# A gated-linear-attention block on one core: weight parts of w_in kept in DRAM after the first block of tokens, and w_o's scaled rows prepared in the last block

## The chip, the cores and the metric

One core of one Trainium2 chip runs the whole program. The metric is the device time of one execution in microseconds; the time of a kernel is the median of its runs. The core's engines are TensorE (PE, with its weight loads as PEld), VectorE (DVE), ScalarE (ACT), GpSimd (POOL) and SyncE (SP), which here issues nearly all transfers, and 16 DMA engines behind the queues.

## The reference, cut to what matters

One layer over 2048 latent tokens of width 1024, with 256 context tokens before them. Attention is gated linear attention in both directions, 4 heads with keys of 128 and values of 256, in chunks of 64 tokens; a two-layer MLP of width 4096 with a squared ReLU follows.

```python
def gla_mixer(a_ctx, a_lat, w_in, w_a1, w_a2, b_a, g_head, w_o, need_ctx):
    def project(a):
        q, k, v, r = jnp.split(a @ w_in, [GLA_DK, 2 * GLA_DK, 2 * GLA_DK + GLA_DV], axis=-1)
...
    def finish(o, r):
        B, T = o.shape[:2]
        o = head_rmsnorm(o, g_head).reshape(B, T, GLA_DV).astype(r.dtype)
        return (o * jax.nn.silu(r)) @ w_o
...
    h_lat = h_lat + mod_l[2] * o_lat
    h_lat = h_lat + mod_l[5] * sqrelu_mlp(modulate(rmsnorm(h_lat, norm2_g[i]), mod_l[3], mod_l[4]), mlp_w1[i], mlp_w2[i])
```

`w_in` is 1024 x 3072, `w_o` 1024 x 1024. `g_head` scales the rows of `w_o`, and the residual factor `mod_l[2]` its columns. The vectors `mod_l` come from a product with `ada_w` (1024 x 6144).

## The kernel before

Every product of two float32 matrices is made of three products of halves (`mm3`, L83 to L86): each operand X is split into a high part, X rounded to the matmul's float32 form by an ACT cast, and a low part, X minus its high part. L84 multiplies high by high, L85 and L86 high by low and low by high. A weight that goes into a product therefore needs two operations after its load: the cast and the subtraction.

The program has a start (modulation vectors, first tokens), attention's first stage, its second stage, and the MLP. The first stage (the loop over `seq`, L443) goes backwards over four blocks of tokens; block 0 holds the context and two halves of 256 latent tokens, blocks 1 to 3 two halves each. In each block it goes over the 4 heads. A head takes three pieces of `w_in`, each 1024 x 256, through `load_piece`: "qk" (L451), "v" (L464) and "r" (L550). On PE a head runs as follows: keys and queries of both halves (`kqps`), a transpose of the decayed keys (`ptk`, L502) that waits for DVE's `kr` (L497), the values of the first half (`vps`), the transpose for the second half, its values, and then for each 128 tokens the state update `pu_`, the gate product `rps` and the output `pov`. `pov` waits for DVE's `st` (L579).

`load_piece` is called 48 times, so each of the 12 pieces of `w_in` is loaded and split four times, once for each block. A call loads two halves of 512 KB (`wraw`), casts each on ACT (L343, `wh`) and subtracts on POOL (L345, `wl`); only the very first half is subtracted on DVE. The tiles `wh` and `wl` have two buffers each, `wraw` has four.

Beside the heads, DVE adds up products of `ada_w` for the modulation vectors (`awp` into `acc`, L627 to L631, six rows of 128 x 512 for each head, from the second head on to the twelfth).

At the start of the second stage (L668 to L680) `w_o` is loaded in eight tiles of 128 x 1024 (`wor`), multiplied on DVE by the rows' head factor `gh` and the columns' residual factor `g1t` (L676), cast on ACT (L677) and subtracted (L678) on DVE and POOL in turn. In the same stretch the output of chunk 0, the last one of the backward pass, is finished (`finish0`, L433; `turn0` with its transposes `pt`, L104), and PE multiplies it by `w_o` (`yp`). Then the second stage goes over the chunks: `front` makes a chunk's attention output (`st` L702, `pov`), and the projection by `w_o` and what prepares the MLP follow.

A list scheduler puts each engine's instructions in order when the program is built; pools with a fixed number of buffers set when a load may be issued. All loads here go through SP's queue, in SP's order.

Of the kernel before, what the change touches and what calls it, by code (L numbers as in the profile page):

```python
# [8 lines left out]
F32 = mybir.dt.float32  # L9
# [4 lines left out]
ALU = mybir.AluOpType  # L14
# [3 lines left out]
P = 128  # L18
D = 1024
ND = D // P  # L20
# [3 lines left out]
NH = 4  # L24
HK = 128
HV = 256
# [11 lines left out]
def kernel(  # L38
# [21 lines left out]
    nc = tc.nc  # L60
# [3 lines left out]
    w_in, w_a1, w_a2, b_a, w_o = w_in[0], w_a1[0], w_a2[0], b_a[0], w_o[0]  # L64

    cmn = ctx.enter_context(tc.tile_pool(name="cmn", bufs=1))
    dram = ctx.enter_context(tc.tile_pool(name="dram", bufs=1, space=DRAM))
# [10 lines left out]
    hs_d = dram.tile([NB, 7, 2, P, NFP, 256], F32, name="hs_d")  # L78
    wt_d = dram.tile([4, NFP, P, 512], F32, name="wt_d")
    g_d = dram.tile([2, P, D], F32, name="g_d")  # L80


    def mm3(ps, sh, sl, mh, ml, start, stop, skip=False):  # L83
# [58 lines left out]
    ab_sh1, ab_sc1, n1g, n2g, gh, ab_sh2, ab_sc2 = (vec[:, 2 + i] for i in range(NV - 2))  # L142
# [6 lines left out]
    def held(shape, dtype, name, n):  # L149
        return [hold.tile([P] + shape, dtype, tag="hb", name=name) for _ in range(n)]  # L150
# [10 lines left out]
    with ExitStack() as sa:  # L161
# [7 lines left out]
        one = sa.enter_context(tc.tile_pool(name="a_one", bufs=1))  # L169
# [45 lines left out]
        for half in range(2):  # L215
            pada = pm.tile([P, 2, hk_, 4], F32, tag="m", name="pada")
            for part in range(2):
# [4 lines left out]
                for q_ in range(2):  # L222
                    c0 = part * D + half * 512 + q_ * 256
# [18 lines left out]
                for j in range(hk_):  # L242
# [9 lines left out]
                                           op0=ALU.add, op1=ALU.mult)  # L252
# [75 lines left out]

        n_piece = [0]

        def load_piece(cols):
            n_piece[0] += 1
            wh = wp.tile([P, ND, 256], F32R, tag="wh", name="wh")
            wl = wp.tile([P, ND, 256], F32R, tag="wl", name="wl")
            for half in range(2):
                raw = ld.tile([P, ND // 2, 256], F32, tag="ld", name="wraw")
                n = 256 // len(cols)
                for i, c0 in enumerate(cols):
                    nc.sync.dma_start(
                        raw[:, :, i * n:(i + 1) * n],  # L340
                        w_in[half * 512:(half + 1) * 512, c0:c0 + n].rearrange("(k p) e -> p k e", p=P))
                hs = wh[:, half * 4:half * 4 + 4, :]
                nc.scalar.copy(hs, raw)  # L343
                eng = nc.vector if (n_piece[0], half) in ((1, 0),) else nc.gpsimd
                eng.tensor_sub(wl[:, half * 4:half * 4 + 4, :], raw, hs.bitcast(F32))  # L345
            return wh, wl


# [25 lines left out]
        blocks = [[("ctx", cx, 0, 0, 1), ("lat", x, 1792, 14, 0), ("lat", x, 1536, 12, 0)]]  # L374
# [13 lines left out]
        def prep(b, hi, xs=None, ready=False):  # L388
            if b < len(blocks):
                _, src, t0, _, mi = blocks[b][hi]  # L390
                prepped[b, hi] = prep_half(src, t0, mi, xs, ready)
# [7 lines left out]
        def ada_finish(part, n, acc):  # L399
            if part in (2, 5):  # L400
                ab = one.tile([1, 512], F32, tag="adl", name="ab", bufs=3)
                e0 = part * D + n * 512
                nc.sync.dma_start(ab, ada_b[e0:e0 + 512].unsqueeze(0))
                nc.vector.tensor_add(acc[0:1], acc[0:1], ab)
                gt_ = one.tile([P, 512], F32, tag="adl", name="gt_", bufs=3)
                pg = pm.tile([P, 512], F32, tag="m", name="pg")
                nc.tensor.matmul(pg, ones, acc, start=True, stop=True)
                nc.scalar.copy(gt_, pg)
                nc.sync.dma_start(g_d[0 if part == 2 else 1, :, n * 512:(n + 1) * 512], gt_)
            else:  # L410
                ks = slice(4 * n, 4 * n + 4)
                pg = pm.tile([P, 4], F32, tag="m", name="pgc")
                for k in range(4):
                    nc.tensor.matmul(pg[:, k:k + 1], acc[:, k * P:(k + 1) * P], ones[:, 0:1], start=True, stop=True)
                if part == 3:
                    nc.vector.tensor_add(b2[:, ks], pg, ab_sh2[:, ks])
                else:
                    nc.vector.tensor_add(s2[:, ks], pg, ab_sc2[:, ks])
                    nc.vector.scalar_tensor_tensor(s2[:, ks], s2[:, ks], 1.0, n2g[:, ks], op0=ALU.add, op1=ALU.mult)
# [21 lines left out]
        acc = None  # L441
        pend = None
        for si, (b, h) in enumerate(seq):  # L443
# [4 lines left out]
                pend = [zchain(prepped[b_, hi][2][0:98], h_) for (b_, hi, h_) in zargs(b, h)]  # L448
            Es = pend
            pend = []  # L450
            wqh, wql = load_piece([h * HK, NH * HK + h * HK])  # L451

            pkq = []
            for hi, (kind, _, _, _, _) in enumerate(blk):
                ah, al, _ = pr[hi]
                ps = pj.tile([P, 2, 2, P], F32, tag="pj", name="kqps")
                for i in range(2 if kind == "lat" else 1):
                    o_ = ps[:, i].rearrange("p c j -> p (c j)")
                    c0 = HK * (1 - i)
                    for k in range(ND):  # L460
                        mm3(o_, wqh[:, k, c0:c0 + HK], wql[:, k, c0:c0 + HK], row(ah, k), row(al, k),
                            k == 0, k == ND - 1)
                pkq.append(ps)
            wvh, wvl = load_piece([2 * NH * HK + h * HV])  # L464
            vt = []

            def project_v(hi):
# [79 lines left out]
            nxt = zargs(*seq[si + 1]) if si + 1 < len(seq) else []  # L547
            if h == NH - 1 and b == 0:
                prep(b + 1, 0)
            wrh, wrl = load_piece([2 * NH * HK + NH * HV + h * HV])  # L550
            nz = 0
            for ci, (hi, kind, j, ch) in enumerate(chs):
                fb, kt, qh, at = ent[hi, j]
# [17 lines left out]
                else:  # L571
                    ah, al, _ = pr[hi]
                    rps = pj.tile([P, HV], F32, tag="pj", name="rps")
                    for k in range(ND):
# [5 lines left out]
                                                   op0=ALU.mult, op1=ALU.subtract)  # L580
# [10 lines left out]
                    else:  # L591
# [6 lines left out]
                                                       op0=ALU.mult, op1=ALU.subtract)  # L598
# [11 lines left out]
                if nz < len(nxt) and ci % 2 == 1 and (h < NH - 1 or ci >= len(chs) - 3):  # L610
                    b_, hi_, h_ = nxt[nz]
                    pend.append(zchain(prepped[b_, hi_][2][0:98], h_))
                    nz += 1
            while nz < len(nxt):
                b_, hi_, h_ = nxt[nz]
# [6 lines left out]
            for part, n, k in ada_q[6 * (si - 1):6 * si] if si else ():  # L622
                if k == 0:
                    acc = one.tile([P, 512], F32, tag="acc", name="acc")
# [7 lines left out]
                if k == ND - 1:  # L632
                    ada_finish(part, n, acc)


    nc.vector.tensor_tensor(ff[:, :, 1:], fl[:, :, :NCC + NCH - 1], fm[:, :, 1:], op=ALU.mult)

# [20 lines left out]
    with ExitStack() as sb:  # L658
# [7 lines left out]
        po = sb.enter_context(tc.tile_pool(name="b_po", bufs=2, space=PSUM, reuse_waits="tile"))  # L666

        wot = [[wo.tile([P, D], F32R, name=f"wo{i}{k}") for i in range(2)] for k in range(ND)]  # L668
        g1t, = held([D], F32, "g1t", 1)
        nc.sync.dma_start(g1t, g_d[0])  # L670
        woh, wol = [], []
        for k in range(ND):
            a_, b_ = wot[k]
            raw, = held([D], F32, "wor", 1)
            nc.sync.dma_start(raw, w_o[k * P:(k + 1) * P, :])
            nc.vector.scalar_tensor_tensor(raw, raw, gh[:, k:k + 1], g1t, op0=ALU.mult, op1=ALU.mult)  # L676
            nc.scalar.copy(a_, raw)  # L677
            (nc.gpsimd if k % 2 else nc.vector).tensor_sub(b_, raw, a_.bitcast(F32))  # L678
            woh.append(a_)
            wol.append(b_)  # L680

# [328 lines left out]
    with ExitStack() as sm:  # L1010
# [54 lines left out]
        for b in range(NB):  # L1065

            acc = [[None] * 4 for _ in range(2)]
            ssqs = [None] * 4
            for i in (1, 2, 6, 5, 3, 7, 4):
                w2 = []  # L1070
                for q in range(2):
                    yps = [py.tile([P, 512], F32, tag="y", name="yp") for _ in range(2)]
                    for fq in range(NFP // FQ):
# [4 lines left out]
                        for f in range(FQ):  # L1078
                            wh, wl = w2[fq * FQ + f]
# [73 lines left out]
```

## Time and profile before

| | |
|---|---|
| median of 3 runs | 2373.53 us (2372.31 to 2375.57) |
| profiled execution | 2376.45 us, span of the trace 2374.7 us |
| mean granted TensorE clock | 0.987 |
| busy share of the span: PE, DVE, ACT, POOL | 96%, 68%, 52%, 22% |
| POOL's subtractions L345 | 236.3 us |
| start / block 0 / blocks 1 to 3 of the first stage | 0 to 62 / 62 to 250 / 250 to 866 us |
| boundary of the stages / second stage / MLP | 866 to 902 / 902 to 1120 / 1120 to 2374.7 us |

A span counts from the first instruction to the last; the execution's own time is 1.75 us more. PE is busy nearly all the time, so the table says only that what can be won lies in PE's idle stretches and in stretches in which it runs at a lower clock; where these are has to be read stage by stage.

### The profile page before, as it was taken

How to read it: one execution, taken by the hardware profiler on the slowest of the kernel's cores; microseconds unless marked ns; L12 is line 12 of the kernel's file. 1: busy time of each engine (PE TensorE's matmuls, PEld its weight loads, DVE VectorE, ACT ScalarE, POOL GpSimd, SP SyncE). 2: the span in 40 equal slices, each digit the busy share in tenths (PEclk: the TensorE clock that was granted, in tenths of full speed). 3: DMA queues.
4: the chain of work that ended last, by engine and by line, in shares of the span. 5: the costliest groups of instructions: out<-in, count | busy, mean ns of one | idle time of the engine just before them, and what ended most of it. 6: DMA issues, size and time to landing. Idle time of an engine off the chain costs nothing.

```text
span 2374.7 us, 36202 instructions
## 1 busy us (share of the span) xinstructions
PE 2286.9 (96%) x13250; PEld 2007.2 (85%) x13250; DVE 1612.1 (68%) x2410; ACT 1232.6 (52%) x2223; POOL 532.4 (22%) x658
## 2 busy tenths in 40 slices
PE   6999999999999989999899999999999999999998
PEld 4899999999999977887688887888878888888886
DVE  7855777777676577877866668766655458745484
ACT  6544454555555556654655556555554345444351
POOL 3333335343443433421000000000002113211131
PEclk9999999999999999999999999999999999999999
DMA  9222454454443256785966668765676557756472
GB/s 280 86 90 89 147 174 147 160 157 141 150 148 109 96 187 222 248 270 196 293 204 211 212 211 271 223 217 187 214 273 245 193 170 269 279 183 221 173 263 83
DMA packets 364635, 456.82 MB, mean 192 GB/s; under 512 B 23164, under 2 KB 268996, under 8 KB 364456
## 3 DMA queue, kind: packets, MB, share of 16 engines
q1 hardware_dynamic: 361784, 446.14, 56.9%
q0 software_dynamic: 2416, 8.07, 1.1%
q8 instruction: 104, 1.70, 0.3%
q14 instruction: 75, 0.61, 0.1%
q10 hardware_dynamic: 256, 0.29, 0.0%
HBM read 318.10 MB, written 136.31 MB: 191 GB/s over the span
## 4 chain that ended last, share of the span: by engine, by line
PE 47%; DMA 2%; DVE 1%; ACT 1%; SPq 0%; issue 0%; POOL 0%; DVEq 0%; POOLq 0%; ACTq 0%
PE yp L86 9%; PE yp L84 9%; PE yp L85 9%; PE pa L84 4%; PE pa L86 4%; PE pa L85 4%; PE pb L84 2%; PE pb L86 2%; PE pb L85 2%; DMA traw<-t_d 1%; PE pc L86 1%; PE pc L84 1%; PE pc L85 1%; DMA w2r<-in_mlp_w_dram 1%; DVE ht L858 0%
## 5 line engine op out<-in xcount | busy, mean ns | idle before, releaser
L84 PE MATMUL yp<-w,hs 128*128 128x512 f32 x896 | 349.2, 390 | 3.5 <-ACT hs L1040 3.5
L86 PE MATMUL yp<-w,hs 128*128 128x512 f32 x896 | 349.4, 390 | 1.1 <-DVE hs L1041 1.1
L85 PE MATMUL yp<-w,hs 128*128 128x512 f32 x896 | 349.0, 390 | 0.0
L1032 POOL TENSOR_TENSOR w<-w2r,w 128x512 fp32r<-128x512 f32 x56 | 99.5, 1776 | 1034.8 <-ACT w L1031 1034.5
L345 POOL TENSOR_TENSOR wl<-wraw,wh 128x1024 fp32r<-128x1024 f32 x95 | 236.3, 2509 | 211.3 <-ACT wh L343 211.3
L1041 DVE TENSOR_TENSOR hs<-hsr,hs 128x1024 fp32r<-128x1024 f32 x112 | 140.2, 1255 | 136.5 <-ACT hs L1040 136.2
L1040 ACT CAST hs<-hsr 128x1024 fp32r<-128x1024 f32 x112 | 117.3, 1049 | 180.3 <-PE yp L86 154.8
L84 PEld LDWEIGHTS yp<-w,hs 128*128 128x128 f32 x896 | 168.7, 188 | 38.9 <-ACT hs L1040 3.9
L86 PEld LDWEIGHTS yp<-w,hs 128*128 128x128 f32 x896 | 168.6, 188 | 36.4 <-DVE hs L1041 1.5
L85 PEld LDWEIGHTS yp<-w,hs 128*128 128x128 f32 x896 | 168.6, 188 | 35.0
L1031 ACT CAST w<-w2r 128x512 fp32r<-128x512 f32 x224 | 137.2, 620 | 106.5 <-PE yp L86 76.8
L1032 DVE TENSOR_TENSOR w<-w2r,w 128x512 fp32r<-128x512 f32 x168 | 134.3, 814 | 59.4 <-ACT w L1031 56.3
L84 PE MATMUL vps<-wh,ah 128*128 128x256 f32 x576 | 165.7, 288 | 0.4 <-DVE qr L509 0.4
L85 PE MATMUL vps<-wl,ah 128*128 128x256 f32 x576 | 165.4, 287 | 0.0
L86 PE MATMUL vps<-wh,al 128*128 128x256 f32 x576 | 164.2, 285 | 0.0
L84 PE MATMUL kqps<-ah,wh 128*128 128x256 f32 x544 | 155.8, 286 | 0.0
L85 PE MATMUL kqps<-al,wh 128*128 128x256 f32 x544 | 154.8, 285 | 0.0
L86 PE MATMUL kqps<-ah,wl 128*128 128x256 f32 x544 | 154.1, 283 | 0.5 <-DVE wl L345 0.5
L84 PE MATMUL pa<-ht,w 128*128 128x512 f32 x384 | 150.4, 392 | 3.7 <-DVE z L981 2.0
L85 PE MATMUL pa<-ht,w 128*128 128x512 f32 x384 | 150.0, 391 | 0.0
L86 PE MATMUL pa<-ht,w 128*128 128x512 f32 x384 | 150.0, 391 | 0.0
L84 PE MATMUL rps<-wh,ah 128*128 128x256 f32 x512 | 146.1, 285 | 0.0
(1278 smaller groups left out, 6385.8 us busy)
## 6 DMA issues: line engine op xcount, KB each, us to landing
hsr<-hs_d SPq DMA_DIRECT2D x112, 512.0 KB, 4.3
w2r<-in_mlp_w_dram SPq DMA_DIRECT2D x160, 256.0 KB, 4.9
wraw<-in_gla_w_in_dram SPq DMA_DIRECT2D x64, 512.0 KB, 3.8
w1r<-in_mlp_w_dram SPq DMA_DIRECT2D x64, 512.0 KB, 4.6
hs_d<-z SPq DMA_DIRECT2D x128, 256.0 KB, 3.9
w2r<-wt_d SPq DMA_DIRECT2D x128, 256.0 KB, 4.0
hs_d<-hs SPq DMA_DIRECT2D x96, 256.0 KB, 3.2
sp_d<-sp SPq DMA_DIRECT2D x60, 384.0 KB, 2.3
```

The source lines that it names most:

```text
L84: nc.tensor.matmul(ps, sh, mh, start=start, stop=False, skip_group_check=skip)
L85: nc.tensor.matmul(ps, sh, ml, start=False, stop=False, skip_group_check=skip)
L86: nc.tensor.matmul(ps, sl, mh, start=False, stop=stop, skip_group_check=skip)
L345: eng.tensor_sub(wl[:, half * 4:half * 4 + 4, :], raw, hs.bitcast(F32))
L1031: nc.scalar.copy(w_[:, 0], raw)
L1032: (nc.vector if f % 4 else nc.gpsimd).tensor_sub(w_[:, 1], raw, w_[:, 0].bitcast(F32))
L1040: nc.scalar.copy(h_[:, 0], raw)
L1041: nc.vector.tensor_sub(h_[:, 1], raw, h_[:, 0].bitcast(F32))
```

## The change

In block 0 a piece is loaded and split as before, and its two parts are stored in DRAM (`wp_d`, 1 MB each). In blocks 1 to 3 the parts are loaded from there, in two transfers of 1 MB, straight into `wh` and `wl`, with no cast and no subtraction. In block 3, tiles of `w_o` (128 x 512, 16 of them) are loaded, multiplied on DVE by head and residual factor and stored in `wo_d`; the second stage loads these and only casts and subtracts them, all subtractions on DVE.

```diff
+    wo_d = dram.tile([ND, P, D], F32, name="wo_d")
+
+    wp_d = dram.tile([NH, 3, 2, P, ND, 256], F32, name="wp_d")
...
-        def load_piece(cols):
+        def load_piece(b, h, i):
             n_piece[0] += 1
             wh = wp.tile([P, ND, 256], F32R, tag="wh", name="wh")
             wl = wp.tile([P, ND, 256], F32R, tag="wl", name="wl")
+            if b > 0:
+                for j, w_ in enumerate((wh, wl)):
+                    nc.sync.dma_start(w_.bitcast(F32), wp_d[h, i, j])
+                return wh, wl
...
                 hs = wh[:, half * 4:half * 4 + 4, :]
                 nc.scalar.copy(hs, raw)
                 eng = nc.vector if (n_piece[0], half) in ((1, 0),) else nc.gpsimd
                 eng.tensor_sub(wl[:, half * 4:half * 4 + 4, :], raw, hs.bitcast(F32))
+            for j, w_ in enumerate((wh, wl)):
+                nc.sync.dma_start(wp_d[h, i, j], w_.bitcast(F32))
             return wh, wl
...
+            if b == len(blocks) - 1:
+                ns = slice(h // 2 * 512, (h // 2 + 1) * 512)
+                if h % 2 == 0:
+                    g1h = one.tile([P, 512], F32, tag="acc", name="g1h")
+                    nc.sync.dma_start(g1h, g_d[0, :, ns])
+                for k in range(4 * (h % 2), 4 * (h % 2) + 4):
+                    fold = one.tile([P, 512], F32, tag="adl", name="fold", bufs=3)
+                    nc.sync.dma_start(fold, w_o[k * P:(k + 1) * P, ns])
+                    nc.vector.scalar_tensor_tensor(fold, fold, gh[:, k:k + 1], g1h, op0=ALU.mult, op1=ALU.mult)
+                    nc.sync.dma_start(wo_d[k, :, ns], fold)
...
-        g1t, = held([D], F32, "g1t", 1)
-        nc.sync.dma_start(g1t, g_d[0])
         woh, wol = [], []
         for k in range(ND):
             a_, b_ = wot[k]
             raw, = held([D], F32, "wor", 1)
-            nc.sync.dma_start(raw, w_o[k * P:(k + 1) * P, :])
-            nc.vector.scalar_tensor_tensor(raw, raw, gh[:, k:k + 1], g1t, op0=ALU.mult, op1=ALU.mult)
+            nc.sync.dma_start(raw, wo_d[k])
             nc.scalar.copy(a_, raw)
-            (nc.gpsimd if k % 2 else nc.vector).tensor_sub(b_, raw, a_.bitcast(F32))
+            nc.vector.tensor_sub(b_, raw, a_.bitcast(F32))
```

On SP, in block 3 of the first stage, the order of one head's transfers before; `wraw` are halves of pieces (a qk half comes as two transfers 128x4x128), `q_d` and `sp_d` are stores of queries and of chunk results:

```order
L519 DMA q_d<-qh 128x2x128 x2
L339 DMA wraw<-in_gla_w_in_dram 128x4x256 x2
L519 DMA q_d<-qh 128x2x128
L339 DMA wraw<-in_gla_w_in_dram 128x4x256 x2
L590 DMA sp_d<-sp 128x768 x3
L339 DMA wraw<-in_gla_w_in_dram 128x4x128 x4
```

And after the change, for a head of block 2 that has no `awp` rows either (the first two `wh`, `wl` are the r piece of this head, the next two the next head's qk, the last two the next head's v):

```order
L530 DMA q_d<-qh 128x2x128 x2
L341 DMA wh<-wp_d 128x2048
L341 DMA wl<-wp_d 128x2048
L530 DMA q_d<-qh 128x2x128 x2
L341 DMA wl<-wp_d 128x2048
L341 DMA wh<-wp_d 128x2048
L601 DMA sp_d<-sp 128x768 x3
L341 DMA wl<-wp_d 128x2048
L601 DMA sp_d<-sp 128x768
L341 DMA wh<-wp_d 128x2048
```

Each head still has three pieces, in six transfers of 1 MB. A part goes straight into a buffer that PE reads, so its transfer waits for PE's last use of the piece two before it; a `wraw` transfer waited for ACT and POOL to be done with the half that was two pieces before.

On DVE, at the boundary between the two stages, before:

```order
L604 COPY o_9075<-pov 128x256
L678 TENSOR_TENSOR wo_11049<-wor,wo_11048 128x1024
L676 SCALAR_TENSOR_TENSOR wor<-wor,vec,g1t 128x1024
L433 SCALAR_TENSOR_TENSOR o_9075<-o_9075,rsr,o_9076 128x256
L676 SCALAR_TENSOR_TENSOR wor<-wor,vec,g1t 128x1024
L678 TENSOR_TENSOR wo_11053<-wor,wo_11052 128x1024
L676 SCALAR_TENSOR_TENSOR wor<-wor,vec,g1t 128x1024
L678 TENSOR_TENSOR wo_11057<-wor,wo_11056 128x1024
L676 SCALAR_TENSOR_TENSOR wor<-wor,vec,g1t 128x1024
L678 TENSOR_TENSOR wo_11061<-wor,wo_11060 128x1024
L702 SCALAR_TENSOR_TENSOR st<-xf_102,ff,st 128x256
```

The same place on DVE after the change (L615, L697, L444 and L721 are the old L604, L678, L433 and L702):

```order
L615 COPY o_8927<-pov 128x256
L697 TENSOR_TENSOR wo_10903<-wor,wo_10902 128x1024
L444 SCALAR_TENSOR_TENSOR o_8927<-o_8927,rsr,o_8928 128x256
L697 TENSOR_TENSOR wo_10905<-wor,wo_10904 128x1024
L697 TENSOR_TENSOR wo_10907<-wor,wo_10906 128x1024
L697 TENSOR_TENSOR wo_10909<-wor,wo_10908 128x1024
L697 TENSOR_TENSOR wo_10911<-wor,wo_10910 128x1024
L697 TENSOR_TENSOR wo_10913<-wor,wo_10912 128x1024
L697 TENSOR_TENSOR wo_10915<-wor,wo_10914 128x1024
L697 TENSOR_TENSOR wo_10917<-wor,wo_10916 128x1024
L721 SCALAR_TENSOR_TENSOR st<-xf_104,ff,st 128x256
```

The multiplications are gone from here (they stand, as 16 smaller ones, in the first two heads of block 3), and the four subtractions that POOL made have come to DVE. PE's order differs in few places, none of them past the boundary.

## Rows read from the trace of the kernel before

**Rows 1.** Three stretches: length, busy PE PEld DVE ACT POOL, clock, DMA share, GB/s.
```profile
62.00:250.00 188.00, 178.96 (x1439) 176.24 (x1438) 117.07 (x199) 94.21 (x177) 68.86 (x120) 0.97 0.29 94
250.00:866.00 616.00, 602.45 (x4976) 597.52 (x4975) 437.45 (x692) 326.29 (x624) 238.56 (x293) 0.99 0.43 140
866.00:902.00 36.00, 27.47 (x110) 20.47 (x109) 32.18 (x37) 19.85 (x36) 15.76 (x13) 0.81 0.76 265
```
**Rows 2.** PE's waits in blocks 1 to 3: us in total, times, longest.
```profile
PE ptk L502 <- DVE kr L497: 7.9, 5, 2.0
PE pov L85 <- DVE st L579: 2.5, 1, 2.5
PE pu L284 <- DVE al L279: 2.2, 4, 0.8
```
**Rows 3.** Timeline of all engines before one wait: start, duration, instruction.
```profile
461.58 5.62 POOL L345 TENSOR_TENSOR wl<-wraw,wh 128x1024 fp32r<-128x1024 f32 x2 [4.12 <-ACT wh L343]
...
462.05 2.90 DVE L631 SCALAR_TENSOR_TENSOR acc<-awp,sil,acc 128x512 f32<-128x512 f32 x1
...
465.58 3.75 DVE L631 SCALAR_TENSOR_TENSOR acc<-awp,sil,acc 128x512 f32<-128x512 f32 x3
...
469.25 0.68 DVE L497 TENSOR_TENSOR kr<-kqps,ge 128x512 f32<-128x512 f32 x1
...
470.07 0.63 PE L502 MATMUL ptk<-ident,kr 128*128 128x128 f32 x4 [1.93 <-DVE kr L497]
```
**Rows 4.** Instructions on `awp`, 40 to 110 us: ns min/median/max.
```profile
L631 DVE SCALAR_TENSOR_TENSOR acc<-awp,sil,acc x7: 739/742/761, 57.9 to 76.6; 128x512 f32<-128x512 f32 x7
```
**Rows 5.** Busy time by stretch, around two waits of PE.
```profile
292.00:300.00 8.00, 6.83 (x45) 6.83 (x46) 6.94 (x13) 4.33 (x9) 0.84 (x1) 0.79 0.61 194
...
470.00:476.00 6.00, 5.92 (x38) 5.96 (x39) 4.71 (x10) 2.13 (x4) 0.00 (x0) 0.72 0.78 234
```
**Rows 6.** Groups by line in blocks 1 to 3: busy us, mean ns.
```profile
L345 POOL TENSOR_TENSOR wl<-wraw,wh 128x1024 fp32r<-128x1024 f32 x74 | 184.7, 2519 | 149.5 <-ACT wh L343 149.5
...
L343 ACT CAST wh<-wraw 128x1024 fp32r<-128x1024 f32 x74 | 77.7, 1054 | 17.9 <-PE kqps L85 16.3 <-POOL flb L493 1.6
```
**Rows 7.** PE's timeline at one head's turns, in block 3.
```profile
734.88 0.28 PE L86 MATMUL rps<-wh,al 128*128 128x256 f32 x1
...
748.17 0.36 PE L84 MATMUL vps<-wh,ah 128*128 128x256 f32 x1
...
762.78 0.28 PE L84 MATMUL rps<-wh,ah 128*128 128x256 f32 x1
```
**Rows 8.** DMA issues of the page: KB each, median us to landing.
```profile
wraw<-in_gla_w_in_dram SPq DMA_DIRECT2D x64, 512.0 KB, 3.8
```
**Rows 9.** Busy time in four us of the boundary.
```profile
872.00:876.00 4.00, 1.56 (x5) 1.26 (x6) 4.00 (x2) 2.29 (x3) 4.00 (x2) 0.68 1.08 409
```
**Rows 10.** PE's waits at the boundary, 866 to 902 us.
```profile
PE pt L104 <- DVE o L433: 3.3, 1, 3.3
PE yp L85 <- DVE wo L678: 2.4, 3, 1.3
PE pov L85 <- DVE st L702: 2.0, 2, 1.7
```
**Rows 11.** Timeline of the boundary: start, duration, instruction.
```profile
871.75 4.86 POOL L678 TENSOR_TENSOR wo<-wor,wo 128x1024 fp32r<-128x1024 f32 x2
871.81 2.58 DVE L433 SCALAR_TENSOR_TENSOR o<-o,rsr,o 128x256 f32<-128x256 f32 x1 [0.72 <-POOL rsr L95]
874.31 3.39 DVE L676 SCALAR_TENSOR_TENSOR wor<-wor,vec,g1t 128x1024 f32<-128x1024 f32 x1
...
877.62 1.21 DVE L678 TENSOR_TENSOR wo<-wor,wo 128x1024 fp32r<-128x1024 f32 x1
878.75 1.27 DVE L676 SCALAR_TENSOR_TENSOR wor<-wor,vec,g1t 128x1024 f32<-128x1024 f32 x1
...
885.62 2.98 DVE L702 SCALAR_TENSOR_TENSOR st<-xf,ff,st 128x256 fp32r<-128x256 f32 x2
```

More of the change, by code (lines that the diff above doesn't have):

```diff
@@ L334, in load_piece @@
             wl = wp.tile([P, ND, 256], F32R, tag="wl", name="wl")
+            if b > 0:
+                for j, w_ in enumerate((wh, wl)):
+                    nc.sync.dma_start(w_.bitcast(F32), wp_d[h, i, j])
+                return wh, wl
+            cols = ((h * HK, NH * HK + h * HK), (2 * NH * HK + h * HV,), (2 * NH * HK + NH * HV + h * HV,))[i]
             for half in range(2):
@@ L337, in load_piece @@
                 n = 256 // len(cols)
-                for i, c0 in enumerate(cols):
+                for m, c0 in enumerate(cols):
                     nc.sync.dma_start(
-                        raw[:, :, i * n:(i + 1) * n],
+                        raw[:, :, m * n:(m + 1) * n],
                         w_in[half * 512:(half + 1) * 512, c0:c0 + n].rearrange("(k p) e -> p k e", p=P))
@@ L450 @@
             pend = []
-            wqh, wql = load_piece([h * HK, NH * HK + h * HK])
+            wqh, wql = load_piece(b, h, 0)
             pkq = []
@@ L463 @@
                 pkq.append(ps)
-            wvh, wvl = load_piece([2 * NH * HK + h * HV])
+            wvh, wvl = load_piece(b, h, 1)
             vt = []
@@ L549 @@
                 prep(b + 1, 0)
-            wrh, wrl = load_piece([2 * NH * HK + NH * HV + h * HV])
+            wrh, wrl = load_piece(b, h, 2)
             nz = 0
```

## Prediction

> **What bounds the kernel now.** The windows by stage come first. TensorE is busy nearly everywhere, so time can come only from where it is idle or runs at a lower clock. In blocks 1 to 3 PE is busy 602.45 of 616 us [rows 1]: 13.55 us idle, and a granted clock of 0.99 whose second decimal hides some 5 us more (below). At the boundary PE is busy 27.47 of 36 us at a clock of 0.81: 8.5 us idle and 0.19 x 36 = 6.8 us lost to the clock, 15.4 together [rows 1]. The DMA engines are at 0.43 in blocks 1 to 3 [rows 1], so there is room for more bytes there.
>
> The second view is the list of PE's waits in blocks 1 to 3. Nearly all of the idle time is behind DVE: 7.9 us in five waits for `kr`, 2.5 us in one for `st`, 2.2 us in four for `al` [rows 2]. DVE is busy only 437 of 616 us [rows 1], so its load does not explain that; what is late is late for a moment.
>
> The third view, the timeline before one of these waits, shows the moment [rows 3]. POOL makes two subtractions L345 between 461.58 and 467.20. In that time one accumulation on DVE takes 2.90 us, and the next three take 3.75 together. Elsewhere the same instruction takes 742 ns [rows 4]. So four accumulations that need 3.0 us took 6.65; `kr`, behind them on DVE, starts at 469.25 instead of some 3.7 us earlier, and PE, which waited 1.93 us, would not have waited at all. The other `kr` waits and the one for `st` look the same: a POOL subtraction of 4.7 to 5.6 us lies over the DVE instructions just before. So instructions on different engines, none of which waits for a result of the other, take longer while they run together. The Trainium skill, "SBUF — State Buffer" (section "SBUF: two separate sides"), states that VectorE and GpSimd share one pair of ports as an exclusive lock, held for a whole instruction, when VectorE has two SBUF inputs and GpSimd reads SBUF. The trace agrees: 2.90 us is about one L345 (2.52 us mean [rows 6]) plus a part of the normal 0.74.
>
> The stalls cost twice. After two of them the granted clock falls: 0.72 over 470 to 476 us, 0.79 over 292 to 300 us [rows 5], that is 0.28 x 6 and 0.21 x 8, 1.7 us lost after each. A third place, at 564 to 572 us, is alike. Three times 1.7 is 5.1 us.
>
> **The change part by part.**
> *Blocks 1 to 3, what goes.* Of 74 POOL subtractions there (184.7 us) and 74 casts on ACT (77.7 us) [rows 6], 72 of each go: POOL loses about 180 us and ACT 76. Neither is time of PE. What it brings is that nothing long is left on POOL: 7.9 for `kr`, 2.5 for `st` and 0.8 of the 2.2 for `al` (the one of the four that lies under a POOL subtraction) are 11.2 us of waits [rows 2], and with them the 5.1 us of low clock. Upper bound 16.3 us. For the lower bound I leave half of the `kr` waits and one low-clock stretch standing (4 + 1.7), which gives 10.6. I take 15, since the row shows a margin of 1.8 us (3.7 against 1.93) for the wait that I worked out.
>
> *Blocks 1 to 3, what is added.* Six transfers of 1 MB for each head in place of raw halves: 36 MB become 72 MB. 140 GB/s over 616 us becomes about 200 [rows 1], far from the 409 that the boundary reaches [rows 9]. The point is when they may start: a part goes straight into a buffer that PE still reads. In one head [rows 7] the r piece can start when `kqps` is done (748) and is needed at 762.78: 14.8 us. The next v piece starts when `rps` is done (735) and is needed at 748.17: 13 us, and its second transfer stands behind a store of the last chunk, an estimated 2 us later (the nine products of the last `pov` and its copy), so 11 us are left. The next qk piece has more than the r piece. No row has a 1 MB transfer. From below: 512 KB land in 3.8 us [rows 8], and 0.52 MB more at 409 GB/s [rows 9] take 1.3, so 5.1 us for the first and 7.7 for two in a row. From above: 3.8 us for 512 KB [rows 8] four times one after the other, 15.2 us, if nothing overlaps. At the boundary's 409 GB/s transfers do overlap (512 KB in 3.8 us alone are 138 GB/s), so I take 7.7; against 11 it is hidden, with 3 us to spare, and so costs nothing. If that cover goes, each head loses what is missing and a low-clock stretch on top. By the fit of the Trainium skill, "DMA: Bandwidth & Descriptors" (section "Anatomy of one DMA"), 2.0 us plus bytes over 436 GB/s, one after the other, two 1 MB transfers take 8.8 us; the sum would be the same, with 2 us to spare in place of 3.
>
> *Block 0.* 24 MB of stores come onto SP's queue. The store of `wl` waits for POOL's subtraction, and behind it stand the raw loads of the piece after next, which wait for the same subtraction anyway. 94 GB/s [rows 1] plus 24 MB in 188 us make about 220. POOL's subtractions stay, and with them the 9 us idle [rows 1]. Cost 0, bounds 3 either way.
>
> *The products of w_o in block 3.* 16 accumulations' worth of DVE, 0.74 us each by the nearest row [rows 4], are 12 us beside a DVE that has 30% free; they stand before and behind `kr` of the second half, which PE needs only after the first half's values, some 7 us, half of the 14.6 from 748.17 to 762.78 [rows 7]. 8 MB of transfers more. Hidden; if three of them delayed a `kr`, it would be by at most 2.2 us a head in the two heads that have them, 4.4 in all.
>
> *The boundary.* Here DVE is what is late: it runs almost without a gap from 874 to 888 [rows 11] and the loads of `w_o`, all issued by then, are not waited for. It loses eight multiplications of 1.27 us (10.2 us) and the three delays by POOL's subtractions: the short L433 takes 2.58 us, a multiplication 3.39, two `st` 2.98 [rows 11], each about 2.1 us too long. It gains four subtractions of 1.21, 4.8 us. Now a tile costs DVE 1.21 us where it cost 1.27 and, for every second one, 1.21 more; casts of the 1.05 us kind [rows 6] run beside them on ACT. PE's waits of 3.3, 2.4 and 2.0 us [rows 10] shrink to about one of 2 us, since chunk 0's last normalization still stands between tile 0 and tile 1. 7.7 less 2 is 5.7 of waits, and of the 6.8 us of low clock about half, 3.4, if that one wait still makes the clock fall. 9.1; I take 8, rounded down for the chunks' loads that come at the same time. Bounds: 0, if loads at a full DMA (409 GB/s, share 1.08 [rows 9]) are what is late next, and 13, if the low clock goes too.
>
> *Sum.* 15 + 0 + 8 = 23 us less than the profiled execution (2376.45, its span plus 1.75): 2353.5. The median of the runs shown lies 2.9 us under that execution, so the time is about 2351.
>
> **The rivals.**
> *Late parts (slower).* The loads of `wh`, `wl` are the next thing that PE waits for. For it speaks that before a raw half was loaded two pieces ahead and that the parts now wait for PE itself; against it the spare 3 us. It decides from the point where two transfers take more than 11 us. At 12.6 us the v piece of each of 12 heads is 1.6 us late, and each such wait costs about 1.2 us of low clock more (1.7 behind waits of 2 us or so): 34 us, less 23, or 11 slower: about 2384. In heads with `awp` rows the queue is fuller (1.5 MB more), so they would go first.
>
> *The boundary gives nothing.* If the transfers of the first chunks and `wo_d` compete at the full DMA share, PE's waits stay and go over to loads: only 15 less, 2358.
>
> *DVE, not POOL.* If the `kr` waits come from `awp` transfers and DVE's own queue, and the long accumulations are waits that the trace counts as work, blocks 1 to 3 give 3 us and the boundary 3: about 2367. Against it: the same instruction has 742 ns without POOL beside it.
>
> *Everything goes.* 16.3 and 13 and 1 in block 0: 2343.
>
> **How the numbers follow.** My forecast (2344 to 2359) has 0.55, everything or more 0.07, the boundary giving nothing 0.1, DVE's own queue 0.1, the parts late in a few heads, so that little is left of the gain (2366 to 2378), 0.08, and late parts throughout 0.1. The likeliest is 2351. The range goes from 2341 to 2372; beyond it lie mostly the late parts. About 0.2% (4.7 us) is what a measurement of this kernel can tell from no change. Faster by more than that has 0.8, within it 0.09, slower 0.11.
>
> **What would show it.** In the changed profile POOL should be busy under 60 us in blocks 1 to 3, an accumulation should take 0.74 us throughout, and PE's waits for `kr` and `st` should be gone, with a clock of 1.00 in those blocks and a first stage about 15 us shorter. At the boundary no PE wait should exceed 2 us but the one for chunk 0. The transfers of parts should land within 8 us of their issue, and no wait of PE or PEld should name `wh` or `wl`. I am wrong if such waits appear, above all `vps` for a DMA, if `kr` waits stay with POOL idle, or if block 0 becomes longer by over 3 us through stores ahead of raw loads.

## The result, and the profile after

The changed kernel takes 2350.91 us (median of 4 runs, 2348.07 to 2353.59) against 2374.55 us (4 runs, 2372.31 to 2377.34): 23.6 us less, a ratio of 0.9899 with a 95% interval of 0.9886 to 0.9911. Its profiled execution took 2349.05 us (span 2347.3), 27.4 us less than the one of before.

To see where, PE's first product of a stage is taken from its timeline in both traces. One border has to be put right first: the table above gives block 0 as 62 to 250 us, but its fourth head runs from 240.8 to 308.5 us. The stretch of [rows 1] called blocks 1 to 3 thus holds the end of block 0; block 1's first pieces are loaded and split there, so the sums over that stretch stand, the name does not. The later landmarks therefore begin with that fourth head.

| from - to, by PE's timeline | before, us | after, us | gain |
|---|---|---|---|
| start to first `kqps` | 50.0 | 52.5 | -2.5 |
| heads 1 to 3 of block 0 | 190.7 | 187.9 | 2.8 |
| block 0's head 4 and blocks 1 to 3 | 627.7 | 609.4 | 18.2 |
| boundary and second stage, to the first `pb` of the MLP | 259.4 | 251.8 | 7.6 |
| the rest (in the MLP) | 1246.9 | 1245.7 | 1.2 |

The first row can't be laid to the change: in the kernels of the experiments below, most of them with the same start, it takes 49.4 to 51.6 us. Of the third row's 18.2 us, 4.3 lie in block 0's fourth head (67.7 to 63.5 us), where block 1's first pieces are split, and 14.0 in blocks 1 to 3 proper.

The windows of the changed kernel, to be read beside [rows 1] (length; busy PE, PEld, DVE, ACT, POOL; clock; DMA share; GB/s):

```profile
62.00:250.00 188.00, 180.53 (x1462) 177.60 (x1462) 117.65 (x202) 96.17 (x182) 67.40 (x122) 0.98 0.59 201
...
250.00:847.00 597.00, 595.66 (x4970) 591.98 (x4969) 372.83 (x705) 267.28 (x552) 51.46 (x221) 1.00 0.63 230
847.00:883.00 36.00, 30.14 (x141) 24.11 (x141) 25.94 (x44) 23.90 (x49) 6.35 (x12) 0.91 0.84 281
```

In the middle row PE is idle for 1.3 us, where it was 13.55, and the granted clock is at 1.00, its upper level, where 5.1 us were lost to it before. POOL's busy time fell from 239 to 51 us; DVE's fell from 437 to 373, although the change takes no work from DVE there and adds 12 us (the products of `w_o`).

PE's waits from 240 to 850 us, against [rows 2]:

```profile
PE pu L288 <- DVE al L283: 0.5, 2, 0.3
PE pov L88 <- DVE xf L581: 0.4, 1, 0.4
PE yp L88 <- ACT wo L696: 0.3, 1, 0.3
PE ptr L274 <- ACT a L279: 0.3, 2, 0.2
```

No wait for `kr` or `st` is left. The same place as in [rows 3], one of the last `kr` of block 1, on DVE and PE's transpose:

```profile
453.03 1.53 DVE L642 SCALAR_TENSOR_TENSOR acc<-awp,sil,acc 128x512 f32<-128x512 f32 x2
...
455.74 0.68 DVE L508 TENSOR_TENSOR kr<-kqps,ge 128x512 f32<-128x512 f32 x1
...
460.06 0.60 PE L513 MATMUL ptk<-ident,kr 128*128 128x128 f32 x4
```

Two accumulations take 1.53 us, and `kr` is done 3.6 us before PE comes to the transpose, which has no idle time in front of it.

The wait for `st` in the kernel before, 2.51 us long, had the same cause. There a scaling (`xt`) takes 2.61 us, where it takes 0.75 elsewhere, and the `st` instruction 2.00 in place of 0.48, both beside POOL's subtractions:

```profile
287.68 5.16 POOL L345 TENSOR_TENSOR wl<-wraw,wh 128x1024 fp32r<-128x1024 f32 x2
```

```profile
288.03 2.61 DVE L212 TENSOR_SCALAR xt<-xt,rsr 128x1024 f32<-128x1024 f32 x1
...
291.12 2.00 DVE L579 SCALAR_TENSOR_TENSOR st<-xb,fb,st 128x256 fp32r<-128x256 f32 x1
```

The transfers of the parts (issue to landing, minimum, median, maximum):

```profile
DMA to landing us min/median/max: 4.8/7.2/10.2
```

The trace has the landing of 19 of these 72 transfers. The seven that were issued first of a pair took 4.8 to 5.9 us (median 5.3), the eleven issued within 0.6 us behind the other part 7.1 to 10.2 (median 8.3). No wait of PE or PEld names a part or its transfer.

At the boundary DVE's eight subtractions follow one another undisturbed, and L444 and the `st` take what they take alone, against [rows 11]:

```profile
852.86 0.48 DVE L444 SCALAR_TENSOR_TENSOR o<-o,rsr,o 128x256 f32<-128x256 f32 x1 [1.78 <-ACT wo L696]
853.26 8.03 DVE L697 TENSOR_TENSOR wo<-wor,wo 128x1024 fp32r<-128x1024 f32 x7
861.21 0.87 DVE L721 SCALAR_TENSOR_TENSOR st<-xf,ff,st 128x256 fp32r<-128x256 f32 x2
```

PE's waits there, 849 to 885 us, against [rows 10], and behind them the window of lowered clock:

```profile
PE pov L88 <- ACT st L720: 2.9, 2, 1.6
PE pt L108 <- DVE o L444: 1.2, 1, 1.2
PE yp L89 <- DVE wo L697: 0.7, 2, 0.6
```

```profile
866.00:874.00 8.00, 6.79 (x24) 5.87 (x25) 4.73 (x11) 3.95 (x11) 1.70 (x3) 0.57 0.49 140
```

The waits for `w_o` and for chunk 0's normalization have shrunk from 5.7 to 1.9 us, and a new pair of 2.9 us has come: the first chunk of the second stage waits for its state on ACT (`st`, L720). Behind it the granted clock is at 0.57, near the lower of its two levels, for 8 us, 3.4 us lost. Over the whole row of the table PE's idle time went from 16.4 to 12.2 us and the loss to the clock from 6.8 to 3.4.

### The profile page after: what moved, and what is told of

Read it like the earlier page. It is cut to its first block, busy times and chain, and to the rows that moved or that the text cites. A ratio compares the mean times of both kernels' runs of the same rounds, so it can differ in the third digit from the quotient of the medians.

```text
span 2347.3 us, 36061 instructions
## 1 busy us (share of the span) xinstructions
PE 2278.7 (97%) x13250; PEld 2001.7 (85%) x13250; DVE 1534.6 (65%) x2422; ACT 1172.6 (50%) x2151; POOL 329.0 (14%) x582
## 4 chain that ended last, share of the span: by engine, by line
PE 50%; issue 4%; DVE 3%; DMA 3%; POOL 1%; ACT 1%; SPq 0%; POOLq 0%; DVEq 0%; ACTq 0%
PE yp L90 9%; PE yp L88 9%; PE yp L89 9%; PE pa L88 4%; PE pa L90 4%; PE pa L89 4%; PE pb L88 2%; PE pb L90 2%; PE pb L89 2%; DMA traw<-t_d 1%; PE pc L90 1%; PE pc L88 1%; PE pc L89 1%; POOL rsr L99 1%; DMA w2r<-in_mlp_w_dram 1%
## 5 line engine op out<-in xcount | busy, mean ns | idle before, releaser
L89 PE MATMUL rps<-wl,ah 128*128 128x256 f32 x512 | 145.8, 285 | 0.0
```

Source lines behind the costliest of these rows:

```text
L89: nc.tensor.matmul(ps, sh, ml, start=False, stop=False, skip_group_check=skip)
```

## The experiments

Two theories were to be told apart. The first: POOL's subtractions hold up DVE, DVE is late with `kr`, `st` and the boundary's tiles, PE idles and its clock falls. The second: it is the work that went away besides (ACT's casts, the raw loads, two operations between a load and its use) or DVE's own queue. Times are medians against the kernel before on the same chip; "stretch" is block 0's fourth head to the end of the first stage (627.7 us before, 609.4 after), "second stage" the row below it in the table (259.4 and 251.8), both from each kernel's own trace.

**Each half of the change alone.** The first kernel has the new `load_piece` and the old second stage:

```diff
+    wp_d = dram.tile([NH, 3, 2, P, ND, 256], F32, name="wp_d")
-        def load_piece(cols):
+        def load_piece(b, h, i):
```

> Only the parts of w_in are kept in DRAM; w_o is prepared as before the change. If the two halves of the change act apart, blocks 1 to 3 become 18 us shorter (18.2 between the traces of before and after) and the boundary stays: about 18 us less than before in all. If the gain at the boundary came from blocks 1 to 3 too (an earlier free POOL or ACT), this one has nearly all of the 24 us. If the blocks' gain hung on w_o's part, it is near 0.

Measured: 2358.47 us against 2377.14, ratio 0.9915 (0.9899 to 0.9930), 18.7 less. The stretch is 609.4, the second stage 259.7: the blocks' gain is all there, the boundary's is not.

The second kernel has the products of `w_o` in block 3 and the old `load_piece`:

```diff
+                    fold = one.tile([P, 512], F32, tag="adl", name="fold", bufs=3)
...
+            nc.sync.dma_start(raw, wo_d[k])
```

> Only w_o's rows are prepared in block 3; w_in is split in every block as before the change. If the halves act apart: about 7 us less than before, all at the boundary. If the 16 products and their transfers cost something in block 3 while POOL still subtracts there (they lie before and behind kr), 2 to 5 us of it are given back in the first two heads of block 3.

Measured: 2374.31 us against 2377.14, ratio 0.9997 (0.9985 to 1.0009): nothing that can be told from no change. The second stage is 251.1 us, the whole of the boundary's gain, but the first head of block 3 takes 51.9 us in place of 44.2, and so the gain is given back, at the upper end of the second case and beyond. Its DVE timeline in that head shows how:

```profile
703.71 1.93 DVE L646 SCALAR_TENSOR_TENSOR fold<-fold,vec,g1h 128x512 f32<-128x512 f32 x1 [1.76 <-DMA fold<-in_gla_w_o_dram]
705.56 0.68 DVE L508 TENSOR_TENSOR kt<-ptk,kt 128x512 fp32r<-128x512 f32 x1
709.83 0.75 DVE L646 SCALAR_TENSOR_TENSOR fold<-fold,vec,g1h 128x512 f32<-128x512 f32 x1 [3.59 <-DMA fold<-in_gla_w_o_dram]
710.50 0.68 DVE L500 TENSOR_TENSOR kr<-kqps,ge 128x512 f32<-128x512 f32 x1
```

Two products of `w_o` wait for their transfers in front of `kr`, the first of them is held up besides (1.93 in place of 0.75 us, under a POOL subtraction), and PE waits 2.08 us for `kr` and later 2.21 us for `xb`. In the full change the same head costs nothing more (44.2 us). The halves are not independent: what the products of `w_o` cost depends on what else happens in that head. Which of the things that go with the other half makes the difference (POOL's subtractions, raw loads, casts) no run separates.

**POOL's or ACT's work put back.** Kernel with POOL's subtractions, on the pieces that have just landed:

```diff
+                for half in range(2):
+                    s_ = slice(half * 4, half * 4 + 4)
+                    junk_ = ld.tile([P, ND // 2, 256], F32, tag="ld", name="wraw")
+                    nc.gpsimd.tensor_sub(junk_, wh[:, s_, :].bitcast(F32), wl[:, s_, :].bitcast(F32))
```

> The changed kernel, and in blocks 1 to 3 POOL makes two subtractions of 128x1024 for each piece that has landed, into a buffer that nobody reads: POOL's work is back, ACT's casts and the raw loads are not. If the waits came from POOL's reads beside DVE's, kr waits return and 12 to 18 of the 24 us are lost, so 6 to 12 us less than before. If the gain came from the casts that ACT no longer makes, or from weights that no longer pass through two operations, nothing is lost: 24 us less than before, with POOL at its old busy time.

Measured: 2400.32 us against 2377.14, ratio 1.0089: 23 slower than before, with a stretch of 654.2 us. Too much for the theory, and POOL's waits say why:

```profile
POOL wraw L345 <- DMA wl<-wp_d: 147.7, 17, 17.9
...
POOL wraw L345 <- DMA wh<-wp_d: 70.7, 16, 17.3
```

POOL, which works in order, stands at the subtraction until the transfer lands, and its small operations for the next states stand behind. That wait is the experiment's own. The same fault is in its counterpart on ACT, which replaces the subtraction by `nc.scalar.copy(junk_, wh[:, s_, :].bitcast(F32))`:

> The changed kernel, and in blocks 1 to 3 ACT makes two casts of 128x1024 for each piece that has landed, into a buffer that nobody reads. By the theory of POOL's reads nothing comes back: about 24 us less than before, at most 3 us lost. If it was ACT that made kr and st late, 10 us or more are lost.

Measured: 2373.30 us, ratio 0.9985 (0.9972 to 0.9999), a stretch of 631.0: 20 us of the gain gone, against the expectation. ACT waits here for transfers:

```profile
ACT wraw L345 <- DMA wh<-wp_d: 88.7, 27, 7.9
```

Neither tells the theories apart in time. So the next two put the work on tiles made in the head itself (`kt`, `qh`, `v_`), with no transfer to wait for:

```diff
+        def extra(b, t):
+            if b > 0:
+                junk_ = ld.tile([P, ND // 2, 256], F32, tag="ld", name="wraw")
+                nc.gpsimd.tensor_sub(junk_.rearrange("p k e -> p (k e)"), t.bitcast(F32), t.bitcast(F32))
```

> The changed kernel, and in blocks 1 to 3 POOL makes six subtractions of 128x1024 for each head, as many as before the change, into a buffer that nobody reads. They read kt, qh and v_ of each half, which are made in the head itself, so POOL waits for no transfer and no transfer is added; the order of all transfers stays. If POOL's reads beside DVE's were what made kr and st late, DVE's busy time in blocks 1 to 3 goes from 378 to 440 us or so, kr waits are back and 10 to 18 us are lost: 6 to 14 less than before. If the gain lay in the casts or the raw loads, nothing is lost.

Measured: 2361.71 us against 2374.07, ratio 0.9951 (0.9937 to 0.9965): 12.4 less than before, so 11.3 of the 23.6 us are lost. The stretch is 618.9 (9.4 more), but no `kr` wait came back: PE waits 4.6 us for `xt` (L216) in place. The subtractions fall elsewhere in the head than the old ones did. Its DVE groups (mean ns behind the busy time), 240 to 845 us:

```profile
L650 DVE SCALAR_TENSOR_TENSOR acc<-awp,sil,acc 128x512 f32<-128x512 f32 x49 | 45.6, 931 | 19.0 <-DMA awp<-in_ada_w_dram 18.4
L552 DVE TENSOR_TENSOR am<-am 128x256 f32<-128x256 f32 x26 | 24.5, 941 | 0.0
...
L514 DVE TENSOR_TENSOR kr<-kqps,ge 128x512 f32<-128x512 f32 x27 | 18.5, 685 | 9.0 <-PE kqps L90 8.9
...
L216 DVE TENSOR_SCALAR xt<-xt,rsr 128x1024 f32<-128x1024 f32 x10 | 7.5, 752 | 13.0 <-POOL rsr L99 13.0
```

And the same groups of the changed kernel, 240 to 850 us:

```profile
L642 DVE SCALAR_TENSOR_TENSOR acc<-awp,sil,acc 128x512 f32<-128x512 f32 x49 | 38.7, 790 | 15.7 <-DMA awp<-in_ada_w_dram 15.0
...
L508 DVE TENSOR_TENSOR kr<-kqps,ge 128x512 f32<-128x512 f32 x27 | 18.5, 684 | 6.6 <-PE kqps L90 6.4
...
L544 DVE TENSOR_TENSOR am<-am 128x256 f32<-128x256 f32 x26 | 10.8, 415 | 0.0
...
L216 DVE TENSOR_SCALAR xt<-xt,rsr 128x1024 f32<-128x1024 f32 x11 | 8.1, 748 | 3.9 <-POOL rsr L99 3.9
```

So POOL's reads hold up what reads two operands from SBUF (the sum `am` 941 against 415 ns, the accumulation 931 against 790), and leave `kr`, which has one operand in PSUM, as it was. The time lost is another matter. `xt` itself is not held up (752 ns); it starts late, 39 to 42 us after the first `kqps` in the last heads of blocks 1 and 2, against 11 to 18 in the changed kernel. The results that nobody reads take buffers from the pool that the loads of these `xt` use too, so this wait is the experiment's own.

With `nc.scalar.copy` in place of the subtraction:

> The same with six copies of 128x1024 on ACT in place of POOL's subtractions (72 in all, some 76 us, as many as the casts that the change took away). If ACT's casts were no part of the cause, at most 3 us are lost: 20 to 24 less than before, and DVE's busy time stays near 378 us. If ACT's time counts too, 6 us or more are lost.

Measured: 2354.91 us against 2374.07, ratio 0.9919 (0.9905 to 0.9932): 19.2 less, so 4.5 of the gain are lost, a little more than expected; the stretch is 613.6, and DVE's busy time is 376 us from 240 to 845, unchanged. `xt` is late here too, by the same use of buffers (38 to 41 us after the first `kqps`), and PE waits 2.3 us for it, so the 4.5 us are not the price of the casts alone. POOL's subtractions cost 6.8 us more than as many copies on ACT; that difference is nearer to what they do than the 11.3 us.

**One part from DRAM, the other made.** Low parts from DRAM, high parts by raw load and cast; the counterpart the other way round:

```diff
+            if b > 0:
+                nc.sync.dma_start(wl.bitcast(F32), wp_d[h, i, 1])
...
                 nc.scalar.copy(hs, raw)
+                if b > 0:
+                    continue
```

> In blocks 1 to 3 only the low part comes from DRAM; the high part is still made by a raw load and ACT's casts. Against the changed kernel ACT has its 72 casts and the raw loads are back, and POOL still has nothing. Same bytes as the changed kernel. By the theory of POOL's subtractions beside DVE, the whole gain stays: 21 to 24 us less than before, no kr waits, DVE's busy time in blocks 1 to 3 as after (about 373). If the casts on ACT were a part of the cause, 5 us or more of the gain are lost.

Measured: 2363.60 us against 2374.92, ratio 0.9949 (0.9929 to 0.9968), a stretch of 620.6: 11.3 us less than before, about half of the gain, though POOL makes no subtraction there. Five `kr` waits are there, 9.8 us. DVE is hardly held up (an accumulation takes 825 ns), but before three of the waits it stands for `awp`, with `kr` behind; before the other two (3.9 us, in block 3) it stands for tiles of `w_o`. One of the three:

```profile
643.57 0.75 DVE L642 SCALAR_TENSOR_TENSOR acc<-awp,sil,acc 128x512 f32<-128x512 f32 x1 [1.86 <-DMA awp<-in_ada_w_dram]
647.75 1.54 DVE L642 SCALAR_TENSOR_TENSOR acc<-awp,sil,acc 128x512 f32<-128x512 f32 x2 [3.43 <-DMA awp<-in_ada_w_dram]
...
650.47 0.68 DVE L508 TENSOR_TENSOR kr<-kqps,ge 128x512 f32<-128x512 f32 x1
```

Here the order of SP's queue has a transfer of 1 MB (`wl`, issued at 638.84) just ahead of three `awp` (from 640.10). So a second way to a `kr` wait exists, the one of the rival "DVE, not POOL". The changed kernel has late `awp` as well: 27 of 56 are issued within 4.5 us behind a part, and of the ten whose landing its trace has, the five behind parts took 7.2 to 8.4 us and the others 2.9 to 4.3. DVE waits 15.0 us for them there, yet no wait for `kr` follows; why not is not shown.

> In blocks 1 to 3 only the high part comes from DRAM; the low part is made by a raw load and POOL's subtraction. ACT has no casts, POOL has its 72 subtractions back. By the theory of POOL's subtractions most of the gain of blocks 1 to 3 is gone (15 us or more), kr waits are back and DVE's busy time there is 435 to 450. A second cost may come on top: POOL now waits for a transfer of 1 MB before it subtracts. If it was ACT's casts, the gain stays.

Measured: 2410.06 us against 2374.92, ratio 1.0152 (1.0123 to 1.0182), a stretch of 675: the second cost that was named is the larger. POOL waits 168 us for `wh`, PE waits twice for POOL's `wl` and 24 us in seven waits for `kr`. It shows how late parts would look, and is no clean measure of the subtractions.

**The boundary's subtractions.** Every second one on POOL again:

```diff
-            nc.vector.tensor_sub(b_, raw, a_.bitcast(F32))
+            (nc.gpsimd if k % 2 else nc.vector).tensor_sub(b_, raw, a_.bitcast(F32))
```

> The changed kernel, with every second subtraction of w_o's tiles at the boundary on POOL, as before the change. If the boundary's 7.6 us came from POOL's reads beside DVE, 4 us or more are lost there; if they came from the eight multiplications that DVE no longer makes there, under 2.

Measured: 2352.67 us against 2374.92, ratio 0.9904 (0.9885 to 0.9924). The second stage is 256.5 us in its trace, 4.6 of the 7.6 lost, which speaks for POOL; the ratio differs from the changed kernel's by 0.0005, less than either interval, so the time alone does not confirm it. Nor is one trace much here: in the traces of this document the same row takes 251.1 to 255.7 us with the new boundary and 255.8 to 259.7 with the old one.

**Fills that read nothing** (they do write the buffer), three on POOL for each half piece:

```diff
+                    for _ in range(3):
+                        nc.gpsimd.memset(junk_, 0.0)
```

> The changed kernel, and in blocks 1 to 3 POOL fills a buffer that nobody reads, three times 128x1024 for each half piece (216 fills of about 0.9 us): POOL is about as busy as before the change, but writes and reads nothing. If it is POOL's reads that DVE waits for, DVE's busy time in blocks 1 to 3 stays near 373 us and an accumulation near 0.74 us; if any access of POOL's holds DVE up, they rise to 435 or more and to over 1 us. The kernel's time may be longer all the same where the small POOL operations stand behind fills.

Measured in one run: 2412.19 us, so more is read from its instructions than from its time. Its groups, 240 to 870 us:

```profile
L345 POOL MEMSET wraw<- 128x1024 f32 x216 | 198.0, 960 | 50.7 <-PE ptr L274 50.2
```

```profile
L216 DVE TENSOR_SCALAR xt<-xt,rsr 128x1024 f32<-128x1024 f32 x10 | 63.0, 6295 | 6.6 <-POOL rsr L99 6.6
L646 DVE SCALAR_TENSOR_TENSOR acc<-awp,sil,acc 128x512 f32<-128x512 f32 x49 | 38.7, 790 | 14.2 <-DMA awp<-in_ada_w_dram 13.6
...
L548 DVE TENSOR_TENSOR am<-am 128x256 f32<-128x256 f32 x24 | 10.0, 416 | 0.0
```

The expectation had two cases and neither fits whole. What reads two operands from SBUF is not held up at all by fills (790 and 416 ns), as in the first; but the scaling `xt`, one operand in SBUF and result there, takes 6295 ns in the mean where it takes 748 in the changed kernel. The mean hides the spread, 0.75 to 34.38 us. The longest lies under 38 fills in a row:

```profile
472.69 34.38 DVE L216 TENSOR_SCALAR xt<-xt,rsr 128x1024 f32<-128x1024 f32 x1
```

```profile
472.52 34.00 POOL L345 MEMSET wraw<- 128x1024 f32 x38
```

`kr` stands behind that scaling on DVE, and PE waits 30.3 us for it, half of what the stretch (669.9 us) loses against the changed kernel's.

**The subtraction moved to DVE, and nothing else.** The kernel before, with one line changed:

```diff
-                eng = nc.vector if (n_piece[0], half) in ((1, 0),) else nc.gpsimd
+                eng = nc.vector
```

> The kernel before, with all subtractions of w_in's pieces on DVE and none on POOL; nothing else of the change. POOL's share is gone, DVE has 95 subtractions of 1.21 us more. By the theory DVE's busy time in blocks 1 to 3 changes little (74 us of hindrance go, some 88 us of work come), but no single instruction is held up: 5 to 12 us less than before. If the kr waits come from what DVE has to do before kr, whoever does it, no gain or up to 5 us slower.

Measured: 2342.89 us against 2374.07, ratio 0.9867 (0.9854 to 0.9881): 31.2 less, far more than expected, and more than the whole change. The raw loads and ACT's casts are those of before. Groups from 240 to 845 us:

```profile
L345 DVE TENSOR_TENSOR wl<-wraw,wh 128x1024 fp32r<-128x1024 f32 x74 | 89.9, 1220 | 18.7 <-ACT wh L343 18.7
...
L631 DVE SCALAR_TENSOR_TENSOR acc<-awp,sil,acc 128x512 f32<-128x512 f32 x47 | 35.1, 746 | 4.5 <-DMA awp<-in_ada_w_dram 3.9
```

DVE has 90 us of subtractions more there, and is busy for 449 us in these 605, where it was 429 before: an accumulation takes 746 ns in place of 1242. PE's waits in the stretch, against [rows 2]:

```profile
PE pu L284 <- DVE al L279: 0.7, 3, 0.3
PE pov L84 <- DVE xf L570: 0.4, 1, 0.4
PE ptk L502 <- DVE kr L497: 0.4, 1, 0.4
```

The stretch is 610.4 us, within 1 us of the changed kernel's; heads 1 to 3 of block 0 take 177.0 where both others need 188 to 191.

**The changed kernel with block 0's subtractions on DVE too**, by the same line:

> The changed kernel, with block 0's subtractions on DVE too, so that POOL makes none in the first stage. DVE is busy 112 of 178 us in block 0, and 23 subtractions of 1.21 us add 28. If POOL's subtractions hold DVE up in block 0 as they did in blocks 1 to 3, 2 to 4 us less than the changed kernel: 25 to 28 less than before. If block 0's waits come from the chain of xf alone, no change against the changed kernel, or 1 to 3 us more.

Measured: 2338.40 us against 2374.07, ratio 0.9850 (0.9837 to 0.9864): 35.7 less, the fastest of all. Heads 1 to 3 of block 0 take 175.5 us, 12.4 less than in the changed kernel, three to six times what was expected; the three waits of `pov` for `xf` (5.7 us) are gone, and the loss to the clock fell from 4.3 to 0.9 us there.

## Why the prediction was right

*The time.* 2351 was forecast and 2350.91 measured. Part of that is luck: against the profiled execution the sum was 23 us and the trace shows 27.4; the profiled run of before lies 1.9 us over its median, that of after 1.9 under its own, and the 2.5 us that the trace of after loses in the start belong to no part of the change, as far as the other kernels show.

*Blocks 1 to 3, what goes: 15, in the trace 18.2.* The mechanism was right and the size low: of the 13.55 us of idle time 12.2 went, and the 5.1 us of low clock went as counted; the last 0.9 us are not accounted for. 16.3 as an upper bound was too low, since it kept three of the four small `al` waits. That was a misreading: in the trace two of the four (0.8 us each) stand behind an `al` of 1.7 us under a POOL subtraction, where one alone takes 0.68, and the four went from 2.2 to 0.5 us.

The cause is shown from two sides. In the kernel before, the DVE instructions just ahead of each of the five `kr` waits and of the one for `st` take 1.8 to 3.6 us longer than alone, beside POOL's subtractions, and the waits are shorter than that, 1.0 to 2.5 us. And moving the subtractions to DVE, with all casts and raw loads in place, gives the same stretch to 1 us, with 0.4 us of waits for `kr` left. The same run bears out the sum, which counted the casts as nothing. Putting subtractions back on POOL shows the longer instructions again, but no `kr` wait, and about half of the 9.4 us that it loses in the stretch are waits for the late `xt`.

*Late parts.* 5.1 us for one part and 7.7 for two, with 11 us of room, were about right: 5.3 and 8.3 us are the medians, 10.2 the longest. "Within 8 us" was too strict for the second part. The fit quoted beside the sum is given by the Trainium skill, "DMA: Bandwidth & Descriptors" (section "Anatomy of one DMA"), for transfers that GpSimd issues, and SP issues these; nothing hung on it. The room was enough: PE waited for no part. What late parts would cost PE no run shows cleanly; in the kernels in which POOL or ACT waited for such a transfer, about 20 us and more were lost.

*DVE, not POOL.* As the cause in the kernel before it falls, though before four of its five `kr` waits DVE stood 0.7 to 1.7 us for `awp` as well; as a mechanism it is there (low parts from DRAM alone: 9.8 us of `kr` waits without POOL's subtractions, behind `awp` and tiles of `w_o`).

*Block 0: 0, in the trace 2.8*, within the bounds given; where the 2.8 come from is open. That its subtractions stay and with them the idle time was right, and worth more than the 9 us read there: 12.4 us when they go, 3.4 of them from the clock.

*The products of w_o: 0.* Right in the full change, and by no wide margin: with POOL's subtractions, raw loads and casts still there they cost 7.7 us in one head, more than the 4.4 given as the most.

*The boundary: 8, in the trace 7.6.* PE's old waits shrank as described, from 7.7 to 2.4 us. The one wait that would make the clock fall came, but not at chunk 0's normalization (1.2 us): `front`'s `st` on ACT is late next (2.9 us). So the idle time gave 4.1 us in place of 5.7, and the clock 3.4 as worked out. How the gain is shared between the multiplications and POOL's subtractions is not settled: one trace gives POOL 4.6 of 7.6, about as much as the row varies by from kernel to kernel, and the times don't separate it.

## What to carry to other kernels

When PE waits for an engine that is busy only 70% of the time, compare the duration of the instructions just ahead of the wait with that of the same instruction elsewhere; one that takes three times as long has a neighbour, and it is the neighbour that has to move. Then try the cheapest move first: here one line that gives the subtraction to the engine it disturbed brought 31 us, the whole change with its round trip through DRAM 24 us, both together 36 us. A half of a change can be worth nothing alone and more in company (`w_o`'s half: some 5 us by the medians, whose intervals overlap, and 7.6 in the trace of the second stage), so halves are measured apart before either is praised. And work that is put back to test a cause must take no buffer that the kernel needs, or its own waits are measured.

## What the runs showed of the hardware

Which DVE instructions POOL holds up depends on both sides. POOL's subtractions, which read SBUF, held up DVE instructions with two operands in SBUF (`am` 941 against 415 ns, an accumulation 931 against 790) and not `kr`, whose one operand is in PSUM (685 against 684). POOL's fills, which read nothing, left the former alone (416 and 790 ns) and held up a scaling with one operand and its result in SBUF: 6295 ns in the mean against 748. A subtraction held such a scaling up too (2.61 us, once, in the kernel before). The Trainium skill, "SBUF — State Buffer" (section "SBUF: two separate sides"), names both cases: an instruction with two SBUF inputs on VectorE contends only with a GpSimd operation that reads SBUF, one in a two-port mode with any. The trace agrees with the first; with the second it agrees if the scaling runs in such a mode, which no run here shows. That one DVE instruction can then wait for many fills in a row (34.38 us under 38 of them, where a fill takes 0.96) I had not expected.
